# Two edits to a hybrid decoder layer: where ten modulation columns are written down, and how the compression matmuls stack their operand

## The chip, the core and the metric

The kernel runs on one core of a Trainium2 chip. The metric is device time in microseconds (us). Five engines run their own instruction streams in order: TensorE (PE; its weight loads are shown as PEld), VectorE (DVE), ScalarE (ACT), GpSimd (POOL), and SyncE (SP), which here only issues DMAs. An instruction that waits holds up everything behind it on its engine.

## The reference

One layer with 512 tokens and a width of 2048. A conditioning vector gives six modulation vectors of 2048. Two head groups work on the modulated input: a gated convolution, and an attention with 8 heads in three branches. One of these branches attends to compressed keys and values.

```python
mod_all = silu(c) @ w_ada + b_ada                     # 6 vectors: sh1, sc1, g1, sh2, sc2, g2
h = modulate(rms_norm(x, norm1_g), sh1, sc1)
u = h @ w_in                                          # convolution, queries, keys, values, gates

def compress(kv, pe, w1, w2):                         # 31 blocks of 32 tokens, one every 16
    blocks = kv[:, :, idx, :] + pe
    flat = blocks.reshape(blocks.shape[:3] + (CMP_LEN * HEAD_DIM,))     # 32 * 128
    return jax.nn.gelu(flat @ w1) @ w2                # 4096 -> 256 -> 128

x = x + g1 * (concat(rms_norm(y_conv), rms_norm(y_attn)) @ w_out)
h = modulate(rms_norm(x, norm2_g), sh2, sc2)
x = x + g2 * (relu(h @ w_ff1) ** 2 @ w_ff2)
return rms_norm(x, normf_g)
```

## The kernel before

**Precision.** A float32 operand is kept as two parts, high and low, whose sum it is. A product takes three matmuls (`mm3`): high x high, high x low, low x high. ACT makes the high part of a weight (`wh`, `hl`), DVE the low one (`wl`, `hl`) by a subtraction, called a split here. A weight blob is 128 x 1024, 512 KB, and comes in through a small ring (`raw`, later `rw`).

**Three programs.** The kernel is recorded in three pieces. In each an `Order` object takes down every operation, plans a begin for each with a table of costs, and then issues them in the order of these begins (`emit`); so all instructions have the line of the recording helper, L137. PE instructions of one lane keep the order in which they were written down. The first program has the input projections, the compression, the convolution, values and queries. The second has attention and, as filler in a lane of its own, `out_conv(m)` for m = 0 to 15: the output projection of the convolution half, one tile of 128 columns each. The third has the output projection of the attention half (`w_oa`, eight steps k) and the feed-forward.

**Slots.** Large tiles live in 29 slots of 128 x 1024 (`mainp`). Within a program the planner hands out slots in the order in which tiles are first written in the recorded code; a later tile gets a later freed slot and waits for its last reader. Slots that matter here: the eight `mix` tiles (normalized convolution tokens, read by every `out_conv`), the `x1` tiles (residual rows, loaded from `xr` and kept), two `cs` tiles and four `wa` tiles of `late_ada`.

**Modulation columns.** One column is two dot products on DVE, each against a 512 KB half of a row of `w_ada`; a dot writes `t` and then its sum is read out into `acc` or `mod`. Most columns are done in the first program. Ten (`NATT`) are done by `late_ada(NATT, 4)` at the end of the second program, and six in the third. A load of `late_ada` goes into `wa[(2k+i) % 4]`, so load n + 4 waits for dot n.

**The end of the second program.** After the attention loop come the normalization of the attention output (`ya`, split into `mixa`), then `late_ada`, then the last `out_conv` tiles, then the first two `w_oa` weights. An `out_conv` tile is 24 matmuls into one of two banks (`pw`), then an update on DVE (`x`, in the code `x1[...]`) that adds the product to the residual rows and frees the bank. Residual tiles are taken at m = 0, 1, 4, 5, 8, 9, 12, 13, each for two values of m; the last, for m = 13 and 15, comes into being in the loop behind `late_ada`.

**Compression.** `compress(which, src)` runs in the first program, once for keys and once for values, in a background lane between projection matmuls. The 32 positions of a block come in two halves of 16; for every position 64 columns (2 kv heads x 32 blocks) are the stationary operand and the 256 columns of `w1` the moving one. High and low parts are tiles of their own (`chi`, `clo`), taken 66 columns wide; the last position of a half, where two more columns would run over the end, has tiles of its own (`edge`). 32 positions x `mm3` add up in one bank.

Of the kernel before, what the change touches and what calls it, by code (L numbers as in the profile page):

```python
# [9 lines left out]
F32 = mybir.dt.float32  # L10
F32R = mybir.dt.float32r
BF16 = mybir.dt.bfloat16
AF = mybir.ActivationFunctionType
OP = mybir.AluOpType
AX = mybir.AxisListType

P = 128
# [18 lines left out]
NATT = 10  # L36
# [8 lines left out]
W_A, W_F, W_V = 64, 128, 134  # L45


def weave(ap, m):

    names = " ".join("xyz"[:len(ap.shape) - 2])  # L50
    return ap.rearrange(f"p {names} (a b i) -> p {names} a i b", b=2, i=m)


def plainly(ap, m):
    names = " ".join("xyz"[:len(ap.shape) - 2])
    return ap.rearrange(f"p {names} (a i b) -> p {names} a i b", b=2, i=m)
# [251 lines left out]
def hybrid_layer(ctx: ExitStack, tc: tile.TileContext, a, out):  # L308
    nc = tc.nc
# [7 lines left out]
    attc = front.enter_context(tc.tile_pool(name="attc", bufs=1))  # L317
    stage = front.enter_context(tc.tile_pool(name="stage", bufs=2))

    def slot(dtype=F32, name="m"):  # L320
        return mainp.tile([P, SLOT], dtype, name=name, tag="m")
# [5 lines left out]
    nc = order = Order(tc, xs[0].tensor.tag, NMAIN, passes=6)  # L327
# [37 lines left out]
    def weights(src, cols=1024, spare=False):  # L365
        raw = next(wraw)[:, :cols]
        nc.sync.dma_start(out=raw, in_=src)
        wh, wl = (slot(F32R, name="sw") for _ in range(2)) if spare else next(whl)
        wh, wl = wh[:, :cols], wl[:, :cols]
        nc.scalar.activation(wh, raw, AF.Copy)  # L370
        nc.vector.tensor_tensor(out=wl, in0=raw, in1=wh.bitcast(F32), op=OP.subtract)
        return wh, wl
# [10 lines left out]
    def mm3(ps, lh, ll, rh, rl, start, stop, more=False, m=0):  # L383
        if m:
            ps, rh, rl = plainly(ps, m), weave(rh, m), weave(rl, m)
        nc.tensor.matmul(ps, lh, rh, start=start, stop=False, skip_group_check=more)
        nc.tensor.matmul(ps, lh, rl, start=False, stop=False, skip_group_check=more)
        nc.tensor.matmul(ps, ll, rh, start=False, stop=stop, skip_group_check=more)
# [136 lines left out]
    for n, v in enumerate((sq[:, 0], sq[:, 1], sx[:, 0])):  # L525
        for t in range(NQ):
            nc.tensor.matmul(total[:, t * P:(t + 1) * P], v[:, t * P:(t + 1) * P], ones, start=n + t == 0,
                             stop=n == 2, skip_group_check=True)
# [122 lines left out]
    for s, (name, k) in enumerate(steps[:-1]):  # L651
        grp = 0 if name == "w_kv" else 1
        first = k == 0 or (k, grp) in ((3, 0), (8, 1))
        last = k == NK - 1 or (k, grp) in ((2, 0), (7, 1))
        if first:
            ps = [bank() for _ in range(8)]
        wh, wl = w
        cols = [slice(n * P, (n + 1) * P) for n in range(8)]
        if s < 3:

            for ww, j in ((wh, 0), (wl, 0), (wh, 1)):
                for n, c in enumerate(cols):
                    nc.tensor.matmul(plainly(ps[n], W_A), ww[:, c], weave(hs[k][:, j], W_A),
                                     start=first and ww is wh and j == 0, stop=last and j == 1)
# [50 lines left out]
    def other():  # L715
        return next(others)

    def late_ada(n, slots):
        c2 = [pair(name="cs") for _ in range(2)]
        for i in range(2):  # L720
            nc.sync.dma_start(out=c2[i], in_=csd[i])
        wa = [slot(name="wa")[:, :1024] for _ in range(slots)]
        for k in range(n):
            m, acc = behind.pop(0), next(accs)
            for i in range(2):
                w = wa[(2 * k + i) % slots]
                nc.sync.dma_start(out=w, in_=a["w_ada"][2 * m + i])
                dot(w, i, acc, m, c2, temp(name="dot").bitcast(BF16))
# [41 lines left out]
    nc.sync.dma_start(out=cw2, in_=a["vec"][:, V_END:])  # L770

    attc.tile([P, 56], F32, name="fill")
    edges = [[attc.tile([P, 66], F32R, name=f"edge{i}{j}") for j in range(2)] for i in range(2)]
    for e in edges:
        for x in e:
            nc.vector.memset(x[:, 64:].bitcast(F32), 0.0)

    def compress(which, src):
        pe = cw2[:, which * 32:which * 32 + 32]
        w2 = [cw2[:, 64 + (which * 2 + i) * P:64 + (which * 2 + i + 1) * P] for i in range(2)]  # L780
        parts = []
        for hf in range(2):
            t = slot(name="ct")
            tv = t[:, :1024].rearrange("p (l g n) -> p l g n", g=NG, n=32)
            n = 32 - hf
            for g in range(NG):
                nc.vector.tensor_tensor(
                    out=tv[:, :, g, :n],
                    in0=src[g].rearrange("p (n l) -> p l n", l=16)[:, :, hf:],
                    in1=pe[:, hf * 16:hf * 16 + 16, None].to_broadcast([P, 16, n]), op=OP.add)  # L790
            if hf:
                nc.vector.memset(tv[:, :, :, 31:], 0.0)
            hi = slot(F32R, name="chi")
            lo = slot(F32R, name="clo")
            nc.scalar.activation(hi, t, AF.Copy)
            nc.vector.tensor_tensor(out=lo, in0=t, in1=hi.bitcast(F32), op=OP.subtract)
            last = edges[hf]
            nc.scalar.activation(last[0][:, :64], t[:, 960:], AF.Copy)
            nc.vector.tensor_tensor(out=last[1][:, :64], in0=t[:, 960:], in1=last[0][:, :64].bitcast(F32), op=OP.subtract)
            parts.append((hi, lo))  # L800
            if hf:
                w = weights(a["cmp_w1"][which * 8], spare=True)
            yield
        pc = other()
        for blk in range(8):
            wh, wl = w
            hi, lo = parts[blk // 4]
            for j in range(4):
                l = blk * 4 + j
                s = slice(j * 256, (j + 1) * 256)  # L810
                m = slice((l % 16) * 64, (l % 16) * 64 + 66)
                ch, cl = (hi[:, m], lo[:, m]) if l % 16 < 15 else edges[blk // 4]
                mm3(pc[:66, :256], ch, cl, wh[:, s], wl[:, s], l == 0, l == 31, m=W_F)
            if blk < 7:
                w = weights(a["cmp_w1"][which * 8 + blk + 1], spare=True)
            yield
        hid = temp([P, 256], name="hid")[:64]
        tt = temp([P, 256], name="htt")[:64]
        nc.scalar.activation(hid, pc[:64, :256], AF.Copy)
        nc.vector.tensor_tensor(out=tt, in0=hid, in1=hid, op=OP.mult)  # L820
        nc.vector.tensor_scalar(tt, tt, 0.044715, 1.0, op0=OP.mult, op1=OP.add)
        nc.vector.tensor_tensor(out=tt, in0=tt, in1=hid, op=OP.mult)
        nc.scalar.activation(tt, tt, AF.Tanh, scale=math.sqrt(2.0 / math.pi))
        nc.vector.tensor_scalar(tt, tt, 1.0, 0.5, op0=OP.add, op1=OP.mult)
        nc.vector.tensor_tensor(out=hid, in0=hid, in1=tt, op=OP.mult)
        pt = other()
        for i in range(2):
            nc.tensor.transpose(pt[:, i * 64:i * 64 + 64], hid[:, i * P:(i + 1) * P], ident[:64, :64])
        hidt = temp([P, 2, NG, 32], name="hidt")
        nc.scalar.activation(hidt.rearrange("p i g n -> p (i g n)"), pt[:, :P], AF.Copy)  # L830
        yield
        if which == 0:
            pk = other()
            for i in range(2):
                nc.tensor.matmul(pk[:, :64], w2[i], hidt[:, i].rearrange("p g n -> p (g n)"),
                                 start=i == 0, stop=i == 1)
            for g in range(NG):
                split(kslc[g][:, :, :32], pk[:, g * 32:g * 32 + 32])
        else:
            pad = temp([P, 2, NG, P], name="hpad")  # L840
            for i in range(2):
                nc.vector.tensor_copy(pad[:, i].rearrange("p g (r n) -> p g r n", n=32),
                                      hidt[:, i, :, None].to_broadcast([P, NG, NR, 32]))
            for g in range(NG):
                pv = other()
                for i in range(2):
                    nc.tensor.matmul(pv[:, :P], pad[:, i, g], w2[i], start=i == 0, stop=i == 1)
                split(vcmp[:, g], pv[:, :P])
# [6 lines left out]
    for j in range(8):  # L855
# [4 lines left out]
        for i in range(3):  # L860
            n = 3 * j + i
# [145 lines left out]
    nc = tc.nc  # L1007
    temps = cycle(ts)
    nc = order = Order(tc, mix[0].tensor.tag, NMAIN, passes=6)
# [128 lines left out]
    m = 2  # L1138
# [20 lines left out]
    for j in range(8):  # L1159
# [4 lines left out]
        order.keep(mt)  # L1164
        split(mt, y)
        mixa.append(mt)
    late_ada(NATT, 4)
    while m < NK:
        out_conv(m)
        m += 1  # L1170
    oa = [weights(a["w_oa"][k]) for k in range(2)]
    order.emit()
    att.close()
# [3 lines left out]
    nc = order = Order(tc, x1[0].tensor.tag, NMAIN)  # L1177
# [80 lines left out]
    for k in range(8):  # L1258
        wh, wl = oa[k] if k < 2 else hilo(hl_tile(16), raw_blob(a["w_oa"][k]))
        for i in range(8):  # L1260
            s = slice(i * P, (i + 1) * P)
            mm3(pm[i], wh[:, s], wl[:, s], mixa[k][:, 0], mixa[k][:, 1], k == 0, k == 7, m=W_F)
    for i in range(8):
        residual(pm[i][:, whole], i, whole)
        if i % 4 > 1:
            j = i // 4 * 2 + i % 2
# [343 lines left out]
    for f in range(8):  # L1610
# [4 lines left out]
        last = f == 7  # L1615
        for q in range(3 if last else 4):
# [7 lines left out]
            for i, w in enumerate(operands(raw, reset=q == 0, have=early if last and q == 1 else None,  # L1624
                                          add=[a["w_f2"][4 * f + q, b] for b in (0, 3)] if last else None)):
                ch, first, end = CHAIN[i]
# [10 lines left out]
                else:  # L1637
                    u, c, neg, new = {U6: (0, HI, True, True), T5: (1, HI, True, True), B2: (0, LO, False, True),
                                      T7: (1, HI, False, False), B3: (0, HI, False, False),
                                      T4: (1, LO, False, True)}[i]  # L1640
                    if last and i in (U6, T5, T4):
                        t = temp()
# [122 lines left out]
```

## Time and profile before

| what | us |
|---|---|
| median of three runs (2034.81, 2035.2, 2038.98) | 2035.2 |
| the profiled execution itself | 2034.72 |
| its span in the trace | 2032.9 |
| first compression matmul starts | 213.6 |
| last compression matmul starts | 340.2 |
| first `late_ada` dot of the second program starts | 665.72 |
| last `out_conv` tile starts on PE | 701.22 |
| first matmul of the third program (`pf`) starts | 709.30 |

How to read it: all times count from the first instruction of the profiled execution. Busy time of PE is modelled, since matmuls are pipelined; its pace is read from the starts of matmuls that follow each other. A row of the timeline gives start, duration, engine, line, operation, output and inputs by the program's names, shape and count, and in brackets the idle time before it and what ended that.

### The profile page before, as it was taken

What the parts mean: (1) busy time and instruction counts of PE and PEld (TensorE: products, weight loads), DVE (VectorE), ACT (ScalarE), POOL (GpSimd) and SP (SyncE); (2) the same over time, 40 slices, a digit from 0 to 9 for tenths busy, and PEclk for the clock granted to TensorE, in tenths of its full rate; (3) what the DMA queues carried; (4) which work ended last, traced back from release to release, by engine and by line L of the source; (5) the groups of instructions that cost most, each with busy time, mean ns of one, the idle gap of its engine ahead of it and who ended that gap; (6) DMA issues with size and microseconds to landing.
All of it is one profiled execution on the core that took longest, in us unless ns stands there. A gap on an engine that the chain in (4) does not pass through costs nothing.

```text
span 2032.9 us, 37850 instructions
## 1 busy us (share of the span) xinstructions
PE 1986.5 (98%) x14994; PEld 1890.4 (93%) x14994; DVE 1797.9 (88%) x2617; ACT 1037.3 (51%) x1533; POOL 174.4 (9%) x288
## 2 busy tenths in 40 slices
PE   8999999999999699999999999999999999999996
PEld 6888888989888599999999999999999999999996
DVE  8999988888898778988888888888899999999998
ACT  5434333335676137766666666665643333334353
POOL 0000000000000000233222322310000000000000
PEclk9999999999999799999999999999999999999998
DMA  9886778884211973699899889868857556547672
GB/s 376 336 351 242 250 273 323 290 299 154 81 63 63 349 283 135 183 299 259 263 278 266 253 276 279 252 219 318 317 200 259 180 194 249 196 178 268 215 213 104
DMA packets 140929, 487.20 MB, mean 240 GB/s; under 512 B 16976, under 2 KB 21584, under 8 KB 140752
## 3 DMA queue, kind: packets, MB, share of 16 engines
q1 hardware_dynamic: 113360, 392.49, 53.3%
q0 software_dynamic: 26816, 91.24, 17.1%
q8 instruction: 118, 1.93, 0.4%
q10 hardware_dynamic: 576, 1.05, 0.1%
q14 instruction: 59, 0.48, 0.1%
HBM read 415.51 MB, written 69.21 MB: 238 GB/s over the span
## 4 chain that ended last, share of the span: by engine, by line
PE 86%; DVE 7%; DMA 4%; issue 2%; ACT 2%; SPq 0%; DVEq 0%; ACTq 0%
PE pf L137 59%; PE ps L137 20%; PE pw L137 2%; DMA wa<-in_w_ada 2%; DVE t L137 2%; PE pv L137 2%; PE s L137 2%; DVE xt L137 1%; PE pt L137 1%; DVE hl L137 1%; DVE wl L137 1%; DVE sacc L137 1%; DMA x<-in_xt 0%; DMA g<-gt 0%; DVE x L137 0%
## 5 line engine op out<-in xcount | busy, mean ns | idle before, releaser
L137 PE MATMUL pf<-tk,hl 128*128 128x256 f32 x10656 | 1194.2, 275 | 3.8 <-DVE t L137 3.4
L137 PEld LDWEIGHTS pf<-tk,hl 128*128 128x128 f32 x10656 | 1192.6, 192 | 4.7 <-ACT hl L137 2.7
L137 ACT ACTIVATE hl<-rw 128x1024 fp32r<-128x1024 f32 x264 | 280.1, 1062 | 314.3 <-PE pf L137 308.5
L137 DVE TENSOR_TENSOR hl<-rw,hl 128x1024 fp32r<-128x1024 f32 x264 | 322.0, 1221 | 50.3 <-ACT hl L137 49.8
L137 ACT ACTIVATE hl<-sg 128x1024 fp32r<-128x1024 f32 x183 | 194.5, 1063 | 215.2 <-PE pf L137 205.6
L137 ACT ACTIVATE wh<-raw 128x1024 fp32r<-128x1024 f32 (+1 forms) x106 | 112.3, 1059 | 228.6 <-PE ps L137 153.8
L137 DVE TENSOR_TENSOR hl<-sg,hl 128x1024 fp32r<-128x1024 f32 x153 | 187.1, 1223 | 33.2 <-ACT hl L137 32.4
L137 PE MATMUL ps<-h_m,wh 128*128 128x512 f32 x720 | 215.5, 379 | 0.0
L137 PE MATMUL ps<-h,wh 128*128 128x512 f32 x560 | 166.8, 384 | 3.4 <-ACT h L137 2.6
L137 PEld LDWEIGHTS ps<-h_m,wh 128*128 128x128 f32 x720 | 135.3, 189 | 19.3 <-DVE h_m L137 0.2
L137 DVE TENSOR_TENSOR wl<-raw,wh 128x1024 fp32r<-128x1024 f32 (+1 forms) x106 | 130.1, 1227 | 26.2 <-ACT wh L137 25.7
L137 PE MATMUL ps<-h_m,wl 128*128 128x512 f32 x360 | 136.5, 379 | 0.0
L137 DVE CUSTOM_DVE_ANT_0 t<-wa,cs,acc 128x1024 bf16<-128x1024 f32 x96 | 123.2, 1284 | 12.0 <-DMA wa<-in_w_ada 11.1
L137 DVE CUSTOM_DVE_ANT_0 t<-wa,cs,vec 128x1024 bf16<-128x1024 f32 x96 | 123.0, 1282 | 7.1 <-DMA wa<-in_w_ada 6.6
L137 PEld LDWEIGHTS ps<-h,wh 128*128 128x128 f32 x560 | 106.3, 191 | 20.8 <-ACT h L137 4.2
L137 DVE TENSOR_TENSOR sg<-sg,rw 128x1024 f32<-128x1024 f32 x92 | 112.5, 1223 | 2.3
L137 DVE TENSOR_TENSOR xt<-xt,pf 128x512 f32<-128x512 f32 x152 | 101.7, 682 | 12.2 <-PE pf L137 12.0
L137 POOL DMA_DIRECT2D g<-gt x180 | 96.9, 550 | 116.7 <-issue 53.7
L137 PE MATMUL ps<-h,wl 128*128 128x512 f32 x280 | 103.0, 380 | 0.0
L137 PE MATMUL pw<-mix,wh 128*128 128x512 f32 x256 | 83.6, 394 | 18.2 <-DVE x L137 18.2
L137 POOL DMA_DIRECT2D rw<-in_w_f x30 | 26.3, 876 | 652.9 <-ACT hl L137 524.2
L137 PEld LDWEIGHTS ps<-h_m,wl 128*128 128x128 f32 x360 | 68.1, 189 | 9.4
(244 smaller groups left out, 2268.1 us busy)
## 6 DMA issues: line engine op xcount, KB each, us to landing
rw<-in_w_f SPq DMA_DIRECT2D x260, 512.0 KB, 4.8
wa<-in_w_ada SPq DMA_DIRECT2D x192, 512.0 KB, 6.3
tk<-g SPq DMA_DIRECT2D x114, 512.0 KB, 6.2
g<-gt POOLq DMA_DIRECT2D x180, 256.0 KB, 7.0
raw<-in_w_conv SPq DMA_DIRECT2D x32, 512.0 KB, 4.5
rw<-in_w_f POOLq DMA_DIRECT2D x30, 512.0 KB, 6.2
sg<-in_w_f POOLq DMA_DIRECT2D x30, 512.0 KB, 5.5
raw<-in_w_kv SPq DMA_DIRECT2D x16, 512.0 KB, 6.4
```

Source lines behind the costliest of these rows:

```text
L137: x.i, x.eng, x.call = len(self.nodes), eng, (lambda: real(*args, **kw))
```

## The change

Two edits. In `compress`, high and low parts of 8 positions go into one tile `cstk`, alternating in runs of 64 columns, so that one stationary operand of 128 columns holds a position's high part in its first and the low part in its last 64. It is multiplied with the high and with the low part of `w1`: two matmuls per position. The rows of the bank from 64 on, the low tokens' products, are added to the others at the end by a copy and an add; low x low is now part of the sum. At the end of the second program the remaining `out_conv` tiles are written down ahead of `late_ada`.

```diff
-    edges = [[attc.tile([P, 66], F32R, name=f"edge{i}{j}") for j in range(2)] for i in range(2)]
-    for e in edges:
-        for x in e:
-            nc.vector.memset(x[:, 64:].bitcast(F32), 0.0)
...
-            hi = slot(F32R, name="chi")
-            lo = slot(F32R, name="clo")
-            nc.scalar.activation(hi, t, AF.Copy)
-            nc.vector.tensor_tensor(out=lo, in0=t, in1=hi.bitcast(F32), op=OP.subtract)
-            last = edges[hf]
-            nc.scalar.activation(last[0][:, :64], t[:, 960:], AF.Copy)
-            nc.vector.tensor_tensor(out=last[1][:, :64], in0=t[:, 960:], in1=last[0][:, :64].bitcast(F32), op=OP.subtract)
-            parts.append((hi, lo))
+            for n in range(2):
+                s = slot(F32R, name="cstk")
+                sv = s.rearrange("p (l h c) -> p l h c", h=2, c=64)
+                src_ = t[:, n * 512:n * 512 + 512].rearrange("p (l c) -> p l c", c=64)
+                nc.scalar.activation(sv[:, :, 0], src_, AF.Copy)
+                nc.vector.tensor_tensor(out=sv[:, :, 1], in0=src_, in1=sv[:, :, 0].bitcast(F32), op=OP.subtract)
+                parts.append(s)
...
-                m = slice((l % 16) * 64, (l % 16) * 64 + 66)
-                ch, cl = (hi[:, m], lo[:, m]) if l % 16 < 15 else edges[blk // 4]
-                mm3(pc[:66, :256], ch, cl, wh[:, s], wl[:, s], l == 0, l == 31, m=W_F)
+                both_ = parts[l // 8][:, l % 8 * P:l % 8 * P + P]
+                nc.tensor.matmul(plainly(pc[:, :256], W_F), both_, weave(wh[:, s], W_F), start=l == 0, stop=False)
+                nc.tensor.matmul(plainly(pc[:, :256], W_F), both_, weave(wl[:, s], W_F), start=False, stop=l == 31)
...
-        nc.scalar.activation(hid, pc[:64, :256], AF.Copy)
+        nc.scalar.activation(tt, pc[64:, :256], AF.Copy)
+        nc.vector.tensor_tensor(out=hid, in0=pc[:64, :256], in1=tt, op=OP.add)
...
-    late_ada(NATT, 4)
     while m < NK:
         out_conv(m)
         m += 1
+    late_ada(NATT, 4)
```

The planner makes a new order out of this. On SP, at the end of the second program, stood before (`wa` are loads of the ring, `x1_3992` the residual rows of tiles 13 and 15, `rw` loads of the third program):

```order
L137 DMA raw_88<-in_w_oa 128x1024
L137 DMA wa_3988<-in_w_ada 128x1024
L137 DMA wa_3989<-in_w_ada 128x1024
L137 DMA wa_3990<-in_w_ada 128x1024
L137 DMA wa_3991<-in_w_ada 128x1024
L137 DMA wa_3988<-in_w_ada 128x1024
L137 DMA wa_3989<-in_w_ada 128x1024
L137 DMA wa_3990<-in_w_ada 128x1024
L137 DMA wa_3991<-in_w_ada 128x1024
L137 DMA x1_3992<-in_xr 128x2x256 x2
L137 DMA rw_5625<-in_w_oa 128x1024
```

and with the change, on SP at the same place (`wa_3919` to `wa_3922` are the ring; nine loads of the first three stand ahead of these rows, with the residual rows, now `x1_3916`, ahead of all of them):

```order
L137 DMA wa_3922<-in_w_ada 128x1024 x2
L137 DMA wa_3919<-in_w_ada 128x1024
L137 DMA wa_3921<-in_w_ada 128x1024
L137 DMA wa_3920<-in_w_ada 128x1024
L137 DMA wa_3922<-in_w_ada 128x1024
L137 DMA wa_3919<-in_w_ada 128x1024
L137 DMA wa_3921<-in_w_ada 128x1024
L137 DMA wa_3920<-in_w_ada 128x1024
L137 DMA wa_3922<-in_w_ada 128x1024
L137 DMA rw_5555<-in_w_oa 128x1024
L137 DMA rw_5556<-in_w_oa 128x1024
L137 DMA wa_3922<-in_w_ada 128x1024
```

The residual rows moved ahead of the ring, and the ring's fourth buffer moved behind: `wa_3922` has the slot of `mix_252`, the first `mix` tile, and its first load waits for the third matmul of the last `out_conv` tile on PE. It carries loads 4, 8, 12, 16 and 20. The first two rows of the third program's weights stand ahead of load 20.

On DVE, with the change, around the split of the last `out_conv` weight (`wl_93<-raw_89`; `ISA` rows are a dot and its readout, `x1_3905` and `x1_3916` the updates of tiles 14 and 15, `wl_91<-raw_87` the split of the first `w_oa` weight):

```order
L137 ISA t_82,acc_97<-wa_3921,cs_3917,vec_98 128x1024
L137 ISA acc_97 128x1
L137 TENSOR_TENSOR wl_93<-raw_89,wh_92 128x1024
L137 SCALAR_TENSOR_TENSOR x1_3905<-pw_3859,mod_103,x1_3905 128x2x256
L137 TENSOR_TENSOR wl_91<-raw_87,wh_90 128x1024
L137 ISA t_84,mod_103<-wa_3922,cs_3918,acc_95 128x1024
L137 ISA mod_103 128x1
L137 SCALAR_TENSOR_TENSOR x1_3916<-pw_3860,mod_103,x1_3916 128x2x256
L137 ISA t_84,acc_94<-wa_3919,cs_3917,vec_98 128x1024
```

Six dots (1, 2, 3, 5, 6, 7 by their loads) stand ahead of these rows' split, the seventh load's being the one in the first row. Behind them dots follow as 4, 9, 11, 10, 8, then the split of the second `w_oa` weight, then 13, 15, 14, 12, 17, 19, 18, 16, 20. Before, the updates of tiles 13 and 15 stood behind all twenty:

```order
L137 ISA t_80,mod_103<-wa_3991,cs_3987,acc_95 128x1024
L137 ISA mod_103 128x1
L137 SCALAR_TENSOR_TENSOR x1_3992<-pw_3930,mod_103,x1_3992 128x2x256 x2
L137 TENSOR_TENSOR wl_93<-raw_88,wh_92 128x1024
L137 TENSOR_TENSOR hl2176_5648<-rw_5625,hl2176_5648 128x1024
```

and with the change the first weight split of the third program (`hl2176_5578`, step k = 2 of `w_oa`) stands right behind dot 20 on DVE:

```order
L137 ISA t_81,mod_103<-wa_3922,cs_3918,acc_97 128x1024
L137 ISA mod_103 128x1
L137 ISA t_80,mod_103<-wa_3922,cs_3918,acc_95 128x1024
L137 ISA mod_103 128x1
L137 TENSOR_TENSOR hl2176_5578<-rw_5555,hl2176_5578 128x1024
```

So the updates moved ahead of 14 of the dots, and the dots are now the last thing ahead of the third program. From its first row on the third program's order is the same as before.

More of the change, by code (lines that the diff above doesn't have):

```diff
@@ L806, in compress @@
             wh, wl = w
-            hi, lo = parts[blk // 4]
             for j in range(4):
```

## Prediction

> **What bounds the kernel now.** I read the page first, for its span and for who is busy.
>
> ```profile
> span 2032.9 us, 37850 instructions
> PE 1986.5 (98%) x14994; PEld 1890.4 (93%) x14994; DVE 1797.9 (88%) x2617; ACT 1037.3 (51%) x1533; POOL 174.4 (9%) x288
> PE 86%; DVE 7%; DMA 4%; issue 2%; ACT 2%; SPq 0%; DVEq 0%; ACTq 0%
> ```
>
> The profiled execution took 2034.72 us, 1.8 more than its span; the median of the three runs, 2035.2, lies 0.5 above it. I work from 2034.72. TensorE (PE) fills 98% and carries 86% of the chain that ended last, so the two questions are how much PE work the change removes and what becomes of the one place where PE stands still. The windows around that place, with PE, weight loads, VectorE (DVE), ACT and POOL busy, then granted clock, DMA share and GB/s:
>
> ```profile
> 670.00:680.00 10.00, 10.00 (x48) 8.77 (x47) 9.91 (x16) 2.11 (x2) 0.00 (x0) 1.00 0.93 326
> 680.00:690.00 10.00, 3.00 (x14) 2.28 (x13) 9.49 (x14) 1.06 (x1) 0.00 (x0) 0.82 0.98 361
> 690.00:700.00 10.00, 0.00 (x0) 0.00 (x0) 7.60 (x13) 0.00 (x0) 0.00 (x0) 0.50 0.89 307
> 700.00:710.00 10.00, 8.78 (x28) 7.27 (x29) 1.57 (x4) 0.71 (x1) 0.00 (x0) 0.65 1.00 390
> 710.00:720.00 10.00, 10.00 (x48) 8.77 (x47) 7.38 (x9) 3.19 (x4) 0.00 (x0) 1.00 0.88 311
> ```
>
> PE stops at 683, stands for 18 us, and starts again at half clock. The chain of waits says for whom, and SyncE's (SP's) timeline why so late:
>
> ```profile
> 687.93 5.07 DMA wa<-in_w_ada
> ...
> 694.45 4.53 DMA wa<-in_w_ada
> ...
> 699.12 1.28 DVE t L137
> ...
> 700.41 0.68 DVE x L137
> ...
> 701.22 8.24 PE pw L137 x24
> ```
>
> ```profile
> 681.96 12.82 SPq L137 DMA_DIRECT2D wa<-in_w_ada  x8
> 695.91 0.90 SPq L137 DMA_DIRECT2D x<-in_xr  x2
> ```
>
> The last output tile needs the accumulator bank of tile 13. That bank is freed by an update `x`, which needs residual rows `x<-in_xr`; SP issues those behind the last eight `wa` loads, and DVE has the update behind the last dot product. The loads go round a ring of four buffers: load, dot, load.
>
> **Compression.** Its matmuls now, the pace of a run of them, and the feed-forward's, which have the shape that the change gives these:
>
> ```profile
> L137 PEld LDWEIGHTS ps<-sw,chi x120: 134/138/138, 213.6 to 339.7; 128*66 128x66 f32 x120
> L137 PE MATMUL ps<-sw,chi x120: 272/273/325, 213.8 to 339.8; 128*66 128x256 f32 x120
> L137 PE MATMUL ps<-sw,clo x60: 272/273/273, 216.2 to 339.9; 128*66 128x256 f32 x60
> L137 PE MATMUL ps<-sw,edge x12: 272/272/273, 245.4 to 340.2; 128*66 128x256 f32 x12
> 325.30 0.27 PE L137 MATMUL ps<-sw,chi 128*66 128x256 f32 x1
> ...
> 326.50 0.60 PE L137 MATMUL ps<-h_m,wh 128*128 128x512 f32 x2
> L137 PE MATMUL pf<-tk,hl 128*128 128x256 f32 x10656 | 1194.2, 275 | 3.8 <-DVE t L137 3.4
> L137 PEld LDWEIGHTS pf<-tk,hl 128*128 128x128 f32 x10656 | 1192.6, 192 | 4.7 <-ACT hl L137 2.7
> ```
>
> 192 matmuls become 128 (two per position instead of three; 64 positions). Eleven stand between 325.30 and 326.50: 0.109 us each. At 128 columns the pace is 1194.2/10656 = 0.112. So 192 x 0.109 - 128 x 0.112 = 20.9 - 14.3 = **6.6 us less PE work**. Every matmul has a load of its own, and the longer load (192 against 138 ns) hides behind the matmul before it in the feed-forward's row.
>
> The Trainium skill ("TensorE: Matmul & The Clock Gate", section "LDWEIGHTS (loading the stationary operand)") makes a load's time the number of columns over 1.2 in ns, by estimate 52 ns more for 128 than for 66; the trace's 54 agrees. Its section "Part 3: Packing small matmuls" (The mechanism) says that a load overlaps a running matmul only in other row groups. By that, loads of all rows would stand bare: 192 x (0.109 + 0.055) - 128 x (0.112 + 0.107) is by estimate 3.5 us, and the sum below would be 2029.5. The feed-forward's 0.112 at a load of 192 ns speaks against it.
>
> Is PE the limit there, so that the 6.6 us reach the end?
>
> ```profile
> 200.00:300.00 100.00, 99.92 (x519) 87.28 (x518) 88.81 (x121) 39.99 (x51) 0.00 (x0) 1.00 0.69 249
> 300.00:400.00 100.00, 99.68 (x566) 88.84 (x565) 85.75 (x131) 34.28 (x41) 0.00 (x0) 1.00 0.87 314
> 400.00:500.00 100.00, 100.00 (x535) 89.50 (x534) 81.70 (x124) 41.35 (x61) 0.00 (x0) 1.00 0.66 235
> 520.00:630.00 110.00, 109.89 (x618) 93.35 (x617) 106.45 (x318) 83.78 (x238) 0.00 (x0) 1.00 0.17 53
> L137 DVE TENSOR_TENSOR clo<-ct,chi x4: 1210/1214/1231, 208.6 to 276.6; 128x1024 fp32r<-128x1024 f32 x4
> L137 DVE TENSOR_TENSOR xt<-xt,pf 128x512 f32<-128x512 f32 x152 | 101.7, 682 | 12.2 <-PE pf L137 12.0
> ```
>
> PE idles 0.4 us in 300, while DVE has 12 to 18% free and the DMA 13 to 34%. I take the whole 6.6; if loads or DVE cannot follow the faster PE, as little as 0. A split of 1024 columns (1.214) becomes two of 512 (0.682 by the nearest row): 4 x 0.15 = 0.6 us more DVE work. Two adds of 256 columns at the end, each under 0.68, add at most 1.4, and four short edge splits go. Strided halves could cost up to a second 0.68 per piece, 5.5 us, half of the 11 to 18 us that DVE has free in a hundred; all of it lies beside PE, and I count 0.
>
> In attention DVE is busy 106.45 of 110 us with the same operations in another order. At most 3.5 us are there to be won; I take 0 and, lacking a row, let as much be lost.
>
> **The order behind attention.** The two `x<-in_xr` loads now go out before the `wa` loads, so the old wait goes. What comes late instead is read from the order: `wa_3922`, the fourth buffer of the ring, now gets the place of `mix_252`, the first token tile, which the last output tile is the last to read. SP stands before the first `wa_3922` until PE is three matmuls into that tile, and 14 of the 20 dots stand on DVE behind its weights. The next stage's weights `hl` stand behind all of them. Prices:
>
> ```profile
> 685.48 1.22 DVE L137 TENSOR_TENSOR wl<-raw,wh 128x1024 fp32r<-128x1024 f32 x1
> ...
> 689.14 1.28 DVE L137 CUSTOM_DVE_ANT_0 t<-wa,cs,acc 128x1024 bf16<-128x1024 f32 x1
> 690.35 0.08 DVE L137 DVE_READ_ACCUMULATOR2_ANT mod<- 128x1 f32 x1
> 690.35 1.28 DVE L137 CUSTOM_DVE_ANT_0 t<-wa,cs,vec 128x1024 bf16<-128x1024 f32 x1
> 679.60 0.59 PE L137 MATMUL pw<-mix,wh 128*128 128x512 f32 x2
> ...
> 680.25 0.59 PE L137 MATMUL pw<-mix,wh 128*128 128x512 f32 x2
> wa<-in_w_ada SPq DMA_DIRECT2D x22, 512.0 KB, 5.3
> rw<-in_w_oa SPq DMA_DIRECT2D x6, 512.0 KB, 8.4
> raw<-in_w_oc SPq DMA_DIRECT2D x4, 512.0 KB, 4.0
> ```
>
> The last three are issue to landing between 640 and 705: 4.0 for loads that go out one by one, 5.3 in a dense stream. A dot takes 1.3 with its readout, an update 0.7, a split 1.2; three matmuls of 512 columns 0.65, so a tile or a k step of 24 takes 5.2. No row shows this ring started by PE, so each landing lies between 4.0 and 5.3: I take 4.0 where SP has just stood still and 5.3 in the stream. Count from the moment when PE starts the last tile; DVE then has six dots done.
>
> - 0.7: PE frees the place; load 4 goes out, lands at 4.7; dot 4 runs 4.8 to 6.1 (0.1 from landing to start).
> - PE ends the tile at 5.2; its update ends at 6.8, dots 9, 11, 10 at 10.8. Load 8, released by dot 4, lands at 10.2; dot 8 ends at 12.1.
> - Split of the second `w_oa` weight: 12.1 to 13.3. PE, through the first k step at 10.4, wants it at its third matmul, 10.8: **stall 2.5**.
> - Dots 13, 15, 14 end at 17.2. Load 12, released by dot 8, lands at 17.5; dot 12 ends at 18.9. Dots 17, 19, 18 end at 24.0. Load 16 lands at 24.3; dot 16 ends at 25.7.
> - Load 20 (again sparse) lands at 29.8; dot 20 ends at 31.2; the split of `hl` for k = 2 at 32.4. PE wants it at 13.3 + 22 x 0.216 + 0.4 = 18.4: **stall 14.0**.
>
> Both stalls are 16.5 us against 18.2 before. After the old one 24 matmuls took 8.24 where 5.18 is the pace, 3.1 lost at half clock; the new one is long enough for the same, so 3.1 stands on both sides. **The gap shrinks by 1.7, it does not close.** With 5.3 for every landing 3.9 of that go (-2.2); with 4.0 for every one 2.6 more come. Behind it DVE and DMA stand idle often enough to catch up, and the third program's rows are the same in both orders.
>
> The Trainium skill ("TensorE: Matmul & The Clock Gate", section "Part 1: The HAM clock gate") has the half clock end after some 3.4 us of work; by estimate 1.7 us are lost, and the sum would be 2024.9. The old restart's 3.1 decides.
>
> Sum: 2034.7 - 6.6 - 1.7 = **2026.4 us**.
>
> **Rivals.**
> - The gap closes altogether: 2034.7 - 6.6 - 18.2 - 3.1 = 2006.8. For it: the wait that the chain shows is gone. Against it: SP and DVE work in order, and `hl` stands behind dot 20.
> - Slower: the late ring runs at the landings of a full queue, 8.4 as `rw` has it. Place: the five loads of `wa_3922`; price 3 x 4.4 + 2 x 3.1 = 19.4, so 2045.8. It decides from 2.5 us more per landing on, when the gain of 8.3 and another 4.1 are gone. Against it: 8.4 came with six loads at once; here SP waits between them.
> - The compression gains nothing: 2033.0. Either the longer loads stand bare, and 128 x 0.054 (192 less 138 ns) = 6.9 eat the 6.6, or the DMA, at 0.87 of its time in 300 to 400, becomes the limit. Against it: the feed-forward's pace, and PE's idle 0.4.
> - Attention's new order makes DVE, its limit, wait some 5 us more: 2031.4. For it: with 3.5 us idle in 110 nothing covers a wait. Against it: the operations are the same.
>
> **How the numbers follow.** Forecast 0.62, gap closed 0.07, slow ring 0.08, no gain in compression 0.13, attention 0.10. A measurement of this kernel tells 0.2%, 4.1 us, from no change. The forecast, the closed gap and some of the attention case (0.03) are faster: 0.72; the two small cases are the same: 0.20; the slow ring is slower: 0.08. The range goes from 2020.0 (landings at 4.0, attention 3.5 better) to 2034.5 (compression hidden and landings at 5.3), and leaves out the closed gap and the slow ring.
>
> **What would show it.** 128 compression matmuls at 0.112 and the first attention score some 6 us earlier; no wait of `pw` for DVE `x`; a wait of `pf` for DVE `wl` of 2 to 3 us and one for DVE `hl` of 12 to 17, with clock rows of 0.5 there; SP standing about 2 us before one `wa`. I am wrong if PE runs through into `pf`, if the second wait passes 25 us, or if attention starts no earlier.

## The result, and the profile after

The changed kernel takes 2026.91 us (median of four runs, 2025.93 to 2027.89); the kernel before, on the same chip, 2036.83 (four runs, 2034.81 to 2038.98). The ratio is 0.9948, with an interval of 0.9936 to 0.996: 10 us faster, where 8.3 were forecast. The profiled execution took 2027.81 us, its span 2026.0. The page's span, busy times and chain by engine:

```profile
span 2026.0 us, 37738 instructions
PE 1981.0 (98%) x14930; PEld 1884.7 (93%) x14930; DVE 1798.2 (89%) x2615; ACT 1037.5 (51%) x1533; POOL 174.9 (9%) x288
PE 91%; DVE 5%; DMA 2%; issue 2%; ACT 1%; SPq 0%; DVEq 0%; ACTq 0%
```

PE has 5.5 us less work (1986.5 before), still fills 98% of the span, and carries 91% of the chain (86% before). There is still a place where it stands. PE's waits between 500 and 760, in total, times and longest:

```profile
PE pf L137 <- ACT hl L137: 8.8, 1, 8.8
PE pf L137 <- DVE hl L137: 4.0, 1, 4.0
PE pf L137 <- DVE wl L137: 1.7, 1, 1.7
```

The wait of `pw` for `x` (18.2) is gone. In its place PE waits in the next stage, three times, 14.5 in all: 1.7 for the second `w_oa` split, then 8.8 for ACT's high part of `hl` and 4.0 more for DVE's low part. The windows there (PE, weight loads, DVE, ACT, POOL, clock, DMA share, GB/s):

```profile
680.00:690.00 10.00, 9.87 (x46) 8.31 (x44) 7.65 (x11) 1.06 (x1) 0.00 (x0) 1.00 0.51 160
690.00:700.00 10.00, 5.02 (x22) 4.08 (x22) 7.95 (x14) 0.00 (x0) 0.00 (x0) 0.99 0.96 308
700.00:710.00 10.00, 1.22 (x2) 0.50 (x2) 5.46 (x9) 2.82 (x3) 0.00 (x0) 0.50 0.87 333
710.00:720.00 10.00, 9.34 (x29) 7.65 (x30) 5.84 (x8) 1.41 (x2) 0.00 (x0) 0.66 1.03 419
720.00:730.00 10.00, 10.00 (x48) 8.74 (x48) 6.01 (x8) 3.23 (x4) 0.00 (x0) 1.00 1.00 379
```

PE's hole has moved some 10 us later and has become a little smaller; the clock drops to 0.50 in it as before. DVE, whose splits end the first and the last of these waits, is itself idle for a fifth to almost a half of the first four windows, and its timeline says for what:

```profile
683.56 1.29 DVE L137 CUSTOM_DVE_ANT_0 t<-wa,cs,acc 128x1024 bf16<-128x1024 f32 x1 [2.35 <-DMA wa<-in_w_ada]
...
690.26 1.22 DVE L137 TENSOR_TENSOR wl<-raw,wh 128x1024 fp32r<-128x1024 f32 x1
...
695.97 1.29 DVE L137 CUSTOM_DVE_ANT_0 t<-wa,cs,acc 128x1024 bf16<-128x1024 f32 x1
...
703.07 1.28 DVE L137 CUSTOM_DVE_ANT_0 t<-wa,cs,acc 128x1024 bf16<-128x1024 f32 x1
708.17 1.28 DVE L137 CUSTOM_DVE_ANT_0 t<-wa,cs,acc 128x1024 bf16<-128x1024 f32 x1 [3.81 <-DMA wa<-in_w_ada]
709.38 3.49 DVE L137 TENSOR_TENSOR hl<-rw,hl 128x1024 fp32r<-128x1024 f32 x3
```

These are dot 4, the second `w_oa` split, dots 12, 16 and 20, and the first `hl`: the chain that the prediction counted out. DVE waits for `wa` loads, and the split that PE needs stands behind the last dot. The chain of waits has load 4 and the loads of dots 14 and 18, which stand right ahead of dots 12 and 16 (start and length, from issue to landing), and SP's own wait for PE is in its list of waits:

```profile
679.76 3.78 DMA wa<-in_w_ada
...
689.16 5.46 DMA wa<-in_w_ada
...
696.07 5.66 DMA wa<-in_w_ada
```

```profile
SPq L137 <- PE pw L137: 2.7, 1, 2.7
```

One more thing comes late in the same place. ACT makes the first high parts of `hl` as soon as their `rw` loads land:

```profile
704.28 2.25 ACT L137 ACTIVATE hl<-rw 128x1024 fp32r<-128x1024 f32 x2 [19.14 <-DMA rw<-in_w_oa]
```

SP issues these loads at 697.67, behind nineteen loads of the ring. So PE would have stood 8.8 for these loads, as they landed, even if the split had not stood behind dot 20; the split adds the last 4.0.

To see where the time went, three marks cut the span: the first compression product, the first score and the first feed-forward product (first start in each row; a row gives count, duration in ns, first and last start). Before and then after:

```profile
L137 PE MATMUL s<-kslc,q x120: 178/296/481, 514.0 to 626.9; 128*128 128x160 f32 x24, 128*128 128x288 f32 x24, 128*128 128x416 f32 x24, 128*128 128x512 f32 x24
L137 PE MATMUL pf<-tk,hl x10656: 274/275/426, 794.6 to 2010.2; 128*128 128x256 f32 x198
```

```profile
L137 PE MATMUL ps<-sw,cstk x128: 272/275/377, 216.4 to 337.1; 128*128 128x256 f32 x128
L137 PE MATMUL s<-kslc,q x120: 181/297/482, 511.0 to 626.0; 128*128 128x160 f32 x24, 128*128 128x288 f32 x24, 128*128 128x416 f32 x24, 128*128 128x512 f32 x24
L137 PE MATMUL pf<-tk,hl x10656: 275/275/422, 788.3 to 2003.2; 128*128 128x256 f32 x198
```

The same marks in all kernels, as lengths of the four stages in us (each from one profiled execution; the experiments follow below):

| kernel | start | compression and projections | attention and boundary | feed-forward | span |
|---|---|---|---|---|---|
| before | 213.8 | 300.2 | 280.6 | 1238.3 | 2032.9 |
| after | 216.4 | 294.6 | 277.3 | 1237.7 | 2026.0 |
| e9, after again | 215.4 | 294.4 | 277.7 | 1237.5 | 2025.0 |
| e1, compression only | 214.7 | 295.3 | 278.7 | 1236.6 | 2025.3 |
| e2, columns only | 216.1 | 300.4 | 275.5 | 1238.5 | 2030.5 |
| e3, 8 columns | 213.6 | 294.4 | 271.2 | 1241.9 | 2021.1 |
| e4, 6 columns | 214.7 | 296.4 | 268.8 | 1244.7 | 2024.6 |
| e5, a third matmul | 214.6 | 301.2 | 276.2 | 1239.4 | 2031.4 |
| e6, ring of three | 214.4 | 297.6 | 273.6 | 1235.8 | 2021.4 |
| e7, 4 columns early | 213.5 | 296.2 | 269.4 | 1239.8 | 2018.9 |
| e8, 8 columns early | 215.4 | 295.2 | 275.5 | 1238.5 | 2024.6 |
| e10, 2 early, ring of three | 214.2 | 297.3 | 265.4 | 1238.2 | 2015.1 |
| e11, 3 early, ring of three | 213.8 | 294.8 | 261.1 | 1236.4 | 2006.1 |
| e12, as e11, old place | 214.3 | 294.9 | 261.7 | 1238.8 | 2009.7 |

After against before: +2.6 - 5.6 - 3.3 - 0.6 = -6.9. The start holds nothing that the change touches on PE, and kernels with one and the same first program (after, e9, e1, e3, e4, e6) have it between 213.6 and 216.4. So a single pair of profiles can hide 3 us; the first score came only 3.0 earlier because this execution started 2.6 later. A row is also only as good as its execution: e3's took 2022.89, the fastest of four with a median of 2027.71, and e4's 2026.39, where its median is 2023.71.

### The profile page after: what moved, and what is told of

It reads as the page before. It is cut to its first block, busy times and chain, and to the rows that moved or that the text cites. A ratio compares the mean times of both kernels' runs of the same rounds, so it can differ in the third digit from the quotient of the medians.

```text
span 2026.0 us, 37738 instructions
## 1 busy us (share of the span) xinstructions
PE 1981.0 (98%) x14930; PEld 1884.7 (93%) x14930; DVE 1798.2 (89%) x2615; ACT 1037.5 (51%) x1533; POOL 174.9 (9%) x288
## 4 chain that ended last, share of the span: by engine, by line
PE 91%; DVE 5%; DMA 2%; issue 2%; ACT 1%; SPq 0%; DVEq 0%; ACTq 0%
PE pf L137 61%; PE ps L137 21%; PE pw L137 4%; PE pv L137 2%; PE s L137 2%; DVE xt L137 1%; DVE t L137 1%; PE pt L137 1%; DMA wa<-in_w_ada 1%; DVE hl L137 1%; DVE sacc L137 1%; DVE sq L137 0%; DMA x<-in_xt 0%; DMA raw<-in_cmp_w 0%; DVE wl L137 0%
## 5 line engine op out<-in xcount | busy, mean ns | idle before, releaser
L137 DVE CUSTOM_DVE_ANT_0 t<-wa,cs,acc 128x1024 bf16<-128x1024 f32 x96 | 122.8, 1281 | 17.2 <-DMA wa<-in_w_ada 16.5
L137 DVE TENSOR_TENSOR xt<-xt,pf 128x512 f32<-128x512 f32 x152 | 101.6, 682 | 12.1 <-PE pf L137 12.0
```

The source lines that it names most:

```text
L137: x.i, x.eng, x.call = len(self.nodes), eng, (lambda: real(*args, **kw))
```

## The experiments

Ratios are against runs of the kernel before on the same chip, with their interval.

**e1 and e2: each half alone.** e1 is the changed kernel with `late_ada` back in its old place, e2 the kernel before with `late_ada` moved.

```diff
+    late_ada(NATT, 4)
     while m < NK:
         out_conv(m)
         m += 1
-    late_ada(NATT, 4)
```

> The compression part alone; the columns stay where they were before. Theory (PE is the limit while the compression runs, so its 6.6 us reach the end, and the old gap stays): ratio to before 0.9968, about 2028.5 beside 2035.1; first attention score 6 us earlier than before's 513.8; a wait of pw for DVE x of some 18 us stays. Rival A (half of it is lost, since the first score came only 3 us earlier in the changed kernel's profile): ratio 0.9985. Rival B (no gain, the whole difference comes from the columns): 1.000.

> The columns alone, behind the last output tiles; compression as before. Theory (both stalls behind attention together are about 2 us shorter than the old one): ratio 0.9990, about 2033; no wait of pw for x; a wait of pf for wl of about 2 us and for hl of about 13, with clock rows of 0.5. Rival (the compression's gain does not reach the end and this part makes the whole difference): ratio 0.9955.

e1: 0.9959 (0.9946 to 0.9973); the wait of `pw` for `x` is there with 17.2. The gain of the compression reaches the end; rivals A and B of e1 fall, since 0.9985 and 1.000 lie outside the interval. e2: 0.9976 (0.9961 to 0.9991); waits of `pf` for `wl` 1.2 and for `hl` 14.1 (10.3 and 3.8). The move is worth more than the forecast's 1.7: the stage table gives 3 (277.3, 277.7 and 275.5 against 280.6 and 278.7); e2's forecast, 0.9990, lies at the upper end of the interval. The halves, 0.0041 and 0.0024, add up to a little more than the whole, 0.0052, within their intervals.

**e5: a third matmul per position.** Is PE the limit while the compression runs, and what does a matmul cost there?

```diff
                 nc.tensor.matmul(plainly(pc[:, :256], W_F), both_, weave(wl[:, s], W_F), start=False, stop=l == 31)
+                nc.tensor.matmul(plainly(pc[:, 256:], W_F), both_, weave(wl[:, s], W_F), start=l == 0, stop=l == 31, skip_group_check=True)
```

> The changed kernel with a third matmul per position of the compression (128 rows, 128 columns, 256 wide, its sum into the unused half of the bank, which nothing reads): 64 matmuls more. Theory (PE is the limit there, a matmul with a load of its own costs 0.112): stage from PE's 500th matmul to the first score longer by 7.2 us, 390 to 397; ratio to before 0.9983. Rival A (the 192 ns loads stand bare, 0.219 each): 14 us longer, 1.0017. Rival B (something else is the limit there): no longer, 0.9948.

0.9983 (0.9975 to 0.9992), as the theory had it. The stage is 301.2 against a median of 295.0 in the six kernels with the changed first program: 6.2 for 64 matmuls, 0.10 each, a length that varies by 3 between executions. Bare loads, at the expectation's 0.219, would have cost 14. (This kernel's output is not the layer's, although nothing reads the third product; why is open.)

**e3 and e4: fewer columns behind attention.** If `hl` waits for the last dot, fewer dots must let it go earlier. `NATT` is 8 and 6 in place of 10; the rest is done in the next stage.

```diff
-NATT = 10
+NATT = 6
```

> The changed kernel with 8 instead of 10 columns behind attention, so 16 dots there and 4 more in the next stage. Theory (hl stands behind the last dot of the late ring): the last load leaves when the dot of load 12 ends, near 697.3, lands 4 later, and hl ends near 704 instead of 710.7: stall shorter by 6.8, ratio to before about 0.9915 (2018 to 2020; less if the half clock costs less). Rival (the DMA is the limit there: some 33 MB between 660 and 760 in the changed kernel at 350 GB/s need 94 us, PE's own work there is 82): the wait comes back later, ratio 0.994 to 0.995.

> The changed kernel with 6 columns behind attention (12 dots), 8 more dots in the next stage. Theory: the last load leaves near 690.5, hl is ready near 697, when PE wants it; the stall for hl goes, one of about 2 for wl stays, the half clock goes too: 17 us less than the changed kernel, ratio to before 0.987 (2010). Rival 1 (DMA limit as in e3: 12 of the 17 come back as waits on rw loads before 760): ratio 0.992 to 0.993 (2022). Rival 2 (the two columns are not what hl waits for): no change against the changed kernel, 0.995.

e3: 0.9948 (0.9933 to 0.9963), e4: 0.9935 (0.9923 to 0.9948). The wait got shorter as forecast, and the gain is still gone. The stage with the boundary got 6 and 9 us shorter; in e4 there is no wait for `hl` over 0.6. In e3 5.1 of it are left, and all of them are for ACT's high part: fewer dots also let SP reach the `rw` loads sooner, at 695.25 in e3 and 691.53 in e4, so the last dot is not all that `hl` waited for. But the feed-forward got 4 and 7 us longer. PE's waits between 500 and 900 in e4:

```profile
PE pf L137 <- DVE t L137: 3.9, 2, 2.7
PE pf L137 <- DVE sacc L137: 2.8, 1, 2.8
PE pf L137 <- DVE wl L137: 2.3, 1, 2.3
PE pf L137 <- DVE tk L137: 1.7, 3, 1.0
PE pf L137 <- DVE x L137: 1.6, 1, 1.6
```

If loads came late, as my first rival had it, ACT and DVE would wait for them. Between 740 and 880 ACT waits 8.8 us for loads in e4 (10.9 in after) and DVE 0.8 (none in after), so it is not the DMA, though the rival's ratio came out nearly right. All of PE's waits in these lines are for DVE. The windows after, and then in e4, of the feed-forward's start:

```profile
800.00:820.00 20.00, 20.00 (x181) 20.00 (x181) 20.00 (x32) 17.29 (x31) 0.00 (x0) 1.00 0.24 80
820.00:840.00 20.00, 20.00 (x181) 20.00 (x180) 19.75 (x32) 14.66 (x26) 3.47 (x5) 1.00 0.63 163
840.00:860.00 20.00, 19.32 (x173) 19.16 (x172) 19.68 (x29) 12.68 (x20) 8.68 (x14) 1.00 0.95 278
```

```profile
800.00:820.00 20.00, 17.51 (x152) 16.93 (x151) 19.52 (x30) 16.66 (x30) 0.00 (x0) 1.00 0.27 95
820.00:840.00 20.00, 17.32 (x156) 17.16 (x155) 19.99 (x32) 15.15 (x27) 3.48 (x5) 1.00 0.54 131
840.00:860.00 20.00, 18.74 (x168) 18.55 (x167) 19.65 (x31) 11.70 (x18) 8.65 (x14) 1.00 0.98 298
```

The third busy time in a row is DVE's: it is full in both kernels, and with 8 more dots (10.2 us) in the third program PE falls behind, 17.51 where 20.00 stood (e4 entered its feed-forward 8.4 earlier). The dots left a place where DVE idled and went to one where it has nothing left. The table says the same: the kernels with 12 dots in the third program have a feed-forward of 1235.8 to 1239.8, e8 with 8 is no shorter (1238.5), and e3 with 16 and e4 with 20 are longer.

**e6: a ring of three.** Is the late fourth buffer itself the cause?

```diff
-    late_ada(NATT, 4)
+    late_ada(NATT, 3)
```

> The changed kernel with a ring of three buffers behind attention, so that no load waits for a place of the last output tile. Theory (20 dots through a ring set the end, whichever buffer is late): a round of three takes 4.0 to 5.3 for a landing and 1.4 for the dot, 1.8 to 2.2 us per dot; from dot 5 at 675 the last ends at 702 to 708, hl 1.2 later; SP stands before no wa for PE, no stall for wl; 2 to 8 us less stall, ratio 0.991 to 0.994. Rival (the late place alone makes the gap): gap gone, 0.987.

0.9931 (0.9916 to 0.9945). With one buffer less the kernel is faster: no load waits for PE, and the second `w_oa` split comes in time, but `hl` still waits 11.4. The end of DVE's dots in e6, and then the end of the chain of waits:

```profile
702.14 1.28 DVE L137 CUSTOM_DVE_ANT_0 t<-wa,cs,vec 128x1024 bf16<-128x1024 f32 x1 [1.06 <-DMA wa<-in_w_ada]
705.75 1.28 DVE L137 CUSTOM_DVE_ANT_0 t<-wa,cs,acc 128x1024 bf16<-128x1024 f32 x1 [2.33 <-DMA wa<-in_w_ada]
707.98 3.75 DVE L137 TENSOR_TENSOR hl<-rw,hl 128x1024 fp32r<-128x1024 f32 x3 [0.93 <-ACT hl L137]
```

```profile
699.61 7.26 DMA rw<-in_w_oa
...
706.89 1.06 ACT hl L137
...
708.00 1.22 PE pf L137 x2
```

The twenty dots through three buffers end at 707.0, but the split stands another 0.93 for ACT. What PE waits for here is the `rw` load, which SP issues right behind the last load of the ring. So the lateness of one buffer is a part of the gap. The number of dots is the other, by two ways: the split stands behind the last dot on DVE, and `rw` behind the ring's loads on SP.

**e7 and e8: columns into the first program.** `NLATE`, the number of columns left over by the first program, goes from 16 to 12 and 8.

```diff
-NLATE = 16
+NLATE = 12
...
-NATT = 10
+NATT = 6
```

> Four of the sixteen late columns are written down in the first stage, six behind attention, six in the next stage, as in the changed kernel. Theory (e4 closed the gap but gave 8.4 back because its 8 extra dots, 10.2 us of DVE, fell into the feed-forward's start, where DVE is busy 20.00 of 20; the first stage has 12 to 18% of DVE free in 300 us): from attention's end to the first feed-forward product 133 us as in e4, from there to the end 1222.6 as in the changed kernel, PE's 500th matmul to the first score 390 to 391; ratio 0.991 (2018). Rival A (the first stage cannot take them, PE waits 5 to 10 us there): 0.994 to 0.996. Rival B (the DMA is the limit behind attention, 94 us of loads for 82 of PE work): the gap comes back in waits for rw, 0.995.

> Eight late columns in the first stage (16 dots, 20.5 us of DVE where some 45 of 300 are free), four behind attention, four in the next stage. Theory: the gap closes altogether and the feed-forward's start has 4 dots fewer than the changed kernel's 12, so 2 to 4 us less waiting there: ratio 0.988 (2012). Rival A (the first stage is at its limit, 0.87 of the DMA's time in 300 to 400 and 8 MB more): PE waits 8 or more there, 0.993. Rival B (as in e7): 0.993.

e7: 0.9923 (0.991 to 0.9936), e8: 0.9944 (0.9931 to 0.9957). e7's total is near the forecast, its parts are not, and e8 failed; nearest is its rival A, which named waits of 8 or more; there are 12.1, at attention's start. The extra dots do not spread over the first stage: its ring runs at some 2.5 us per dot (16 dots in 40 us), and so they come at its end, and delay attention. From the first score to the last `pv` product, in after and then in e8,

```profile
L137 PE MATMUL pv<-tt,vv x120: 387/393/496, 520.6 to 641.7; 128*128 128x512 f32 x120
```

```profile
L137 PE MATMUL pv<-tt,vv x120: 387/393/492, 537.4 to 658.5; 128*128 128x512 f32 x120
```

attention takes 641.7 - 511.0 = 130.7 us in after and 658.5 - 510.6 = 147.9 in e8 (129.5 before, 137.2 in e7). Among PE's waits in e8 stand there

```profile
PE s L137 <- DVE pc L137: 7.1, 1, 7.1
PE s L137 <- ACT vr L137: 5.0, 1, 5.0
```

**e9 to e11: as many as fit.** In after's last 30 us ahead of attention DVE is busy 20.87,

```profile
480.00:510.00 30.00, 30.00 (x227) 28.87 (x226) 20.87 (x30) 16.13 (x24) 0.00 (x0) 1.00 0.35 114
```

so some 9 us are free: 4 or 6 dots. With a ring of three, e6's times suggest that 14 to 16 dots end about when `hl` is wanted.

```diff
-NLATE = 16
+NLATE = 13
...
-NATT = 10
+NATT = 7
...
-    late_ada(NATT, 4)
+    late_ada(NATT, 3)
```

> The changed kernel unaltered, timed again beside the two that follow. Theory: ratio 0.9948 within its interval of 0.9936 to 0.996; the time of PE's 500th matmul, which was 120.9 in its first profile and 117.7 to 119.9 in the other kernels, lies near 119, since the instructions up to there stand in the same order on PE; if it is 120.9 again, the change itself delays the start.

> Two late columns in the first stage, eight behind attention through a ring of three buffers, six in the next stage. Theory (in e6 dot 15 of 20 ended at 697.9 and hl waited until 709.2; the first stage has 9 us of DVE free between its last dot and attention): 16 dots end near 698, stall 2 to 3 instead of 11.4, half clock gone, attention no longer than 136 to 137, the feed-forward from its first product 1222.6: ratio 0.988. Rival A (each dot moved into the first stage delays attention by 0.8 us as in e7): attention 139, ratio 0.9893. Rival B (the DMA limits the stage behind attention): the gap returns as waits for rw, 0.993.

> As e10 with three columns in the first stage and seven behind attention (14 dots). Theory: no stall behind attention, attention 136 to 138 (6 dots are 7.7 us where 9 are free): ratio 0.9875 to 0.988. Rival A: attention 140 to 141, ratio 0.9885 to 0.989. Rival B as in e10.

e9 repeats the changed kernel: 2026.32 us, 0.9948 (0.9935 to 0.9961). PE's 500th matmul starts at 119.6; counted the same way it is 120.7 in after and 119.7 in e2, which has the old compression, so the change itself does not make the start late. e10 (`NLATE` 14, `NATT` 8): 0.9892 (0.9877 to 0.9907), `hl` waits 3.3 and 0.6. That is the ratio of its rival A but not its mechanism, since attention takes 129.5 and not 139; the wait is a little longer than forecast. e11: 2009.56 us beside 2037.93, **0.9865** (0.9851 to 0.9878). In e11 the hole is gone (windows as above):

```profile
680.00:690.00 10.00, 10.00 (x48) 8.77 (x47) 9.66 (x14) 1.06 (x1) 0.00 (x0) 1.00 0.78 274
690.00:700.00 10.00, 10.00 (x49) 8.72 (x48) 4.43 (x5) 4.23 (x4) 0.00 (x0) 1.00 0.99 379
700.00:710.00 10.00, 10.00 (x48) 8.77 (x47) 6.16 (x9) 1.06 (x1) 0.00 (x0) 1.00 1.03 417
```

Attention takes 130.2 us, as in after, the stage with the boundary is 16 us shorter than there, and the feed-forward has hardly changed. SP issues the first `rw` at 685.14, 12.5 sooner than in after. The DMA is full in the last two windows and PE runs on: the rival of a DMA limit falls here.

**e12: the same in the old place.**

```diff
+    late_ada(NATT, 3)
     while m < NK:
         out_conv(m)
         m += 1
-    late_ada(NATT, 3)
```

> As e11, but the late columns written down ahead of the last three output tiles again, where they stood before the change. Theory (what counts is that 29 buffers hold three and not four of the ring beside the rest, and that 14 dots fit: the residual rows of tiles 13 and 15 then get a buffer that DVE frees near 661 instead of the one left over): no wait of pw for DVE x, no stall behind attention, same as e11, ratio 0.9865 within 0.0015. Rival (the place in the program is what closes the gap): the wait of pw for x is back with 10 us or more, ratio 0.991 or above.

2010.42 us beside 2038.36, 0.986 (0.984 to 0.9881): the same as e11, and no wait of `pw` for `x`. With three buffers the residual rows get one that is free in time: SP issues their last loads at 661.72 and 666.82, where before had 695.91. So where the columns are written down doesn't matter for this pair, once the buffers reach and the dots fit; in the kernel before, and after, moving them only chose which reader got the one late buffer.

## Why the prediction was right

- **Compression, -6.6.** Right in its mechanism, a little too large: the stage shrank by 5.6 (after) and by 5.3 with the median of six kernels, 295.0 against 300.3 in before and e2. The pace is the forecast's, seven matmuls between 325.59 and 326.37, 0.111 each:

```profile
325.59 0.94 PE L137 MATMUL ps<-sw,cstk 128*128 128x256 f32 x7
326.37 0.38 PE L137 MATMUL ps<-h_m,wl 128*128 128x512 f32 x1
```

  PE's busy time in the stage fell by 5.9 (299.80 to 293.87), and its idle time grew by 0.3. PE loses 0.5 to 2.4 there to waits for ACT and DVE (0.7 in after and e1, 0.6 in e9, 2.4 in e6), before 0.2; but e2 with the old compression loses 0.8, so no run shows that the faster PE meets more waits, and where the rest of the 6.6 stays is open. The rival by which loads of all rows stand bare falls: 192 ns loads at 128 columns, and a matmul more cost 0.10 (e5). With it falls, for this shape, the rule of the Trainium skill ("TensorE: Matmul & The Clock Gate", section "Part 3: Packing small matmuls") that a load overlaps only with matmuls of other row groups.
- **Attention in another order, 0.** Nearly right, and inside the 3.5 that it let be lost: 129.5 before, 130.7 after. The 1.2 look real, since e9, e2 and e3 have 130.7 as well and e1, where `late_ada` stands in its old place, 129.5.
- **The chain behind attention.** Right step by step for DVE. PE starts the last tile at 678.9 (its last matmul starts at 683.9, 23 of 0.2165 later). Counted from there, forecast and measured: load 4 lands 4.7 and 4.6, the second `w_oa` split ends 13.3 and 12.6, dot 12 ends 18.9 and 18.4, dot 16 25.7 and 25.5, dot 20 31.2 and 30.6. SP stood 2.7 before the first `wa_3922`, forecast 2. The stalls: 2.5 forecast, 1.7 measured, and 14.0 against 12.8 (e9: 1.8 and 13.3). So the choice of 4.0 for a sparse landing (3.8 measured before dot 4) and 5.3 in the stream (5.5 and 5.7 in the chain of waits) fitted; the second split ended 0.7 earlier than counted, and the dots behind it kept 0.2 to 0.6 of that. What the working left out is `rw` and ACT: the load that it needs for `hl` stands behind the ring on SP as well, and as it landed it would have kept PE 8.8 by itself. That leaving it out did not change the forecast is luck, since the split behind dot 20 came later still.
- **The half clock, 3.1 on both sides.** Right: after the wait PE's timeline has

```profile
710.66 11.71 PE L137 MATMUL pf<-mixa,hl 128*128 128x512 f32 x39 [4.05 <-DVE hl L137]
```

  39 matmuls are 8.4 at the pace of 0.216, so 3.3 are lost. The 1.7 that an estimate from the Trainium skill's "Part 1: The HAM clock gate" gave was too small by half here, too. (With it the sum would be 2026.4 - 1.4 = 2025.0, not 2024.9.)
- **The gap shrinks by 1.7, it does not close.** Right in sign and kind, too small in size. The two stalls were forecast 2 us too long together, so the gap shrank by 3.7 and not by 1.7. From the last `pv` product to the first feed-forward product before takes 151.1 us and after 146.6; attention's 1.2 takes a part back, and the table's stage shows about 3.
- **The sum.** With the measured terms, 5.3 + 3 = 8.3, the forecast's own sum, as the two errors cancel. The difference of the medians, 9.9, is 1.6 more, with an interval of 8.1 to 13.0 that holds both. The forecast started from an execution of 2034.7, while the runs of before have a median of 2036.8, and of up to 2038.4 beside the later kernels. The base was 2.1 low and the gain 1.6 short; that the forecast of 2026.4 came within 0.5 is therefore luck, as it is that the errors of two terms cancel.
- **The range.** Its ends do not follow from the terms that it names: landings at 4.0 and 3.5 off attention make 2026.4 - 2.6 - 3.5 = 2020.3, not 2020.0, and a hidden compression with landings at 5.3 makes 2026.4 + 6.6 + 3.9 = 2036.9, not 2034.5. The measured time lies inside either way.
- **The rivals.** The closed gap, priced at 2006.8, did not come with this change, but e11, in which the gap is closed by a shorter ring and six dots moved ahead of attention, agrees with the price: 2009.6, 27.5 us less than before by its ratio (24.9 to 30.4) against 27.9. The slow ring did not appear; the ring's loads in the chain took 3.8 to 5.7.

## What to carry to other kernels

A load that stands in an in-order queue waits for a buffer, and every load behind it waits too (`rw` in after and e6). Moving it behind other work only handed the late buffer to another reader here: count the buffers first, and try a shorter ring. Work of a side engine that fills no gap must be put where that engine is idle, in microseconds counted from its own windows; the same dots cost nothing (6 of them ahead of attention, 14 behind it) or 0.6 to 0.9 of their length (in attention and at the feed-forward's start). A gain of one half per cent needs several profiles: the start alone varied by 3 us.

## What the hardware showed unexpectedly

- A stop of 1.7 us (after) or 2.3 (e4) left PE's clock at 0.99 and 1.00 in its window. After one of 3.3 in e10 the window reads 0.83, after those of 8.8 (after) and 11.4 (e6) 0.50. In between it went either way: two stops of 2.7 and 2.8 in e4 left 1.00 from 820 to 840 and 0.91 from 760 to 780 (windows of 20 us, the others of 10). The window of e10:

```profile
700.00:710.00 10.00, 9.44 (x37) 7.88 (x37) 4.64 (x6) 2.81 (x3) 0.00 (x0) 0.83 1.03 420
```

- Executions with one and the same first program reach their first compression product between 213.6 and 216.4 us.
